# Strassen's seven products for one pair of column chunks of an MLP's down projection

## The chip, the cores and the metric

The kernel runs on one core of a Trainium2 chip. The metric is the device time of one execution in microseconds; of the runs of the kernel before, the median is 2009.23 us (three runs, 2008.05 to 2010.5).

## The reference

A trunk of two layers on 256 tokens of width 2048, in float32. Layer 0 mixes tokens with a gated MLP, layer 1 with sliding-window attention. Each is followed by the MLP that this change touches:

```
def sq_relu_mlp(x, w_up, w_down):        # w_up [2048, 8192], w_down [8192, 2048]
    return jnp.square(jax.nn.relu(x @ w_up)) @ w_down
...
        x = layer_norm(DEEPNORM_ALPHA * x + mix, ln_g[layer, 0], ln_b[layer, 0])
        x = layer_norm(DEEPNORM_ALPHA * x + sq_relu_mlp(x, mlp_w_up[layer], mlp_w_down[layer]),
                       ln_g[layer, 1], ln_b[layer, 1])
```

## The kernel before

**Weights.** All weights come as tiles [128, 1024] of 512 KB in the order of their use, loaded over SP's queue (L119). Each tile is split ahead of its products into two float32r parts: ScalarE rounds it to `w_hi` (L95), VectorE subtracts to get `w_lo` (L97). A product is then three passes on TensorE: high by high, high by low, low by high. There are 4 places for raw tiles (`RAW`) and, in the MLPs, 10 for split ones (`SLOTS` 5 and `EXTRA_SLOTS` 5); near a layer norm four more are borrowed. `get()` takes the next tile, splits as many tiles ahead as have a place and loads the ones after them; `release()` gives a place back when a tile's products are issued. So a split waits for the products that used its place before, and a load for the split that used its raw place.

**One MLP.** The hidden width 8192 is done in four chunks of 2048. For each chunk, the up products come first: 8 blocks of 256 features (`cols_product`, 4 tiles each, weights stationary, 512 and 256 columns moving; L246, L251). Behind each block `act` adds the two column halves (ScalarE L294, VectorE L300), makes the squared ReLU in one VectorE operation (L381) and splits the result into `hT` (ScalarE L185, VectorE L186). Then the down products: for each of four column chunks of 512 (n = 0 to 3) `rows_product` takes 8 tiles, with `hT` stationary and 512 weight columns moving: 12 matmuls a tile, two K tiles by two token tiles by three passes (L205 to L207). Behind it `residual` adds the two PSUM banks to x (VectorE L353). The last column chunk of the last chunk (`last_rows`) runs token tile 0 ahead of tile 1, so that the layer norm overlaps, and the transposes of the norm run into the next stage's first products (`skewed`).

**PSUM.** The eight banks are two tags of two buffers of two banks: `mm` for products, `aux` for transposes and attention.

**Order.** The framework that builds the program puts the instructions of each engine into a fixed order ahead of time, by what it expects to be ready, and the one that the program names first when several are; each engine then works through its list in order. `keep_in_program_order` pins loads, and the splits around the layer norms, to the program's order.

**Wide buffers.** Two buffers [128, 2048] (tag `wide`) hold the vectors of a layer norm; attention uses them too.

The functions that the change touches:

Of the kernel before, what the change touches and what calls it, by code (L numbers as in the profile page):

```python
# [17 lines left out]
P = 128  # L18
# [5 lines left out]
NFC = DFF // D  # L24
# [11 lines left out]
EXTRA_SLOTS = 5  # L36
# [11 lines left out]
class Weights:  # L48
    """The weights in the order of their use: each tile [128, 1024] is loaded and split
    into two float32r parts (high + low = the float32 value) ahead of its products."""  # L50

    def __init__(self, tc, pool, tiles):
        self.tc, self.nc, self.pool, self.tiles = tc, tc.nc, pool, tiles
# [63 lines left out]
    def dma(self, out, in_):  # L117
        """Loads keep the order of the program: what is used first is loaded first."""
        self.tc.keep_in_program_order(self.nc.sync.dma_start(out=out, in_=in_))  # L119

    def get(self, ahead=None):
# [3 lines left out]
        self.load(self.n_split + RAW)  # L125
# [4 lines left out]
    def release(self):  # L130
        """The oldest tile in use has been used."""
# [6 lines left out]
def trunk(ctx: ExitStack, tc: tile.TileContext, t, out):  # L138
# [8 lines left out]

    def tiles_of(name):
# [3 lines left out]
    order = []  # L152
    ends = {}
    for name in ("win_v", "win_u", "wout", "mlp0", "kv", "wq", "wo", "mlp1"):
        tiles = (mlp_order(tiles_of("up" + name[3:]), tiles_of("down" + name[3:]))
                 if name.startswith("mlp") else tiles_of(name))
        if name == "wo":
            # the last heads' rows of the first two chunks come after the other rows of both
            tiles = tiles[0:6] + tiles[8:14] + tiles[6:8] + tiles[14:]
        order += tiles  # L160
        ends[name] = len(order)
    weights = Weights(tc, wpool, order)
    weights.by_pool = range(ends["kv"] + 4, ends["wq"], POOL_EVERY)
# [25 lines left out]
    def row_steps(stat, apart=False):  # L189
        """[tokens, 512] of both token tiles: activations stationary, weights moving.  # L190
        One step for each weight tile and token tile."""
# [6 lines left out]
        def step(i, tok, hi, lo):  # L198
            for j in range(2):
                k = 2 * i + j  # L200
                wh, wl = hi[:, j * 512:(j + 1) * 512], lo[:, j * 512:(j + 1) * 512]
                xh = stat[:, k, tok * P:(tok + 1) * P]
                xl = stat[:, k, S + tok * P:S + (tok + 1) * P]
                first, last = k == 0, k == NK - 1
# [3 lines left out]
        return ps, [partial(step, i) for i in range(NK // 2)]  # L208

    def rows_product(stat):  # L210
        ps, steps = row_steps(stat)
# [78 lines left out]
    def gather_halves(ps, bias=None):  # L290
        """The sum of the two column halves of cols_product (with a bias per feature)."""
# [7 lines left out]
        full = work.tile([P, 2, S], F32, tag="full", name="full")  # L299
# [16 lines left out]
    def norm_rows(acc, stats, g, b, tok, done):  # L316
        """acc = the layer norm of acc, by column chunks; done(chunk) follows each."""
# [19 lines left out]
    def norm_transposed(acc, stats, g, b, xT, tok):  # L337
        """acc = the layer norm of acc, and its transpose goes to xT in parts."""
# [10 lines left out]
    def residual(acc, ps, n, stats, scale, toks=range(NT)):  # L349
        """acc = scale * acc + ps on column chunk n."""  # L350
# [7 lines left out]
    def last_rows(x, stat, stats, scale, norm, norm_turns=True):  # L358
        """The last column chunk before a layer norm: the norm of token tile 0 runs while
        the products of tile 1 do."""  # L360
        ps, steps = row_steps(stat, apart=True)
# [8 lines left out]
    def borrow(tag, first):  # L370
        if first < len(order):
            weights.borrow(big.tile([P, 4, 2, TILE], F32R, tag=tag, name="lent"), first)

    def mlp(x, xT, norm, loads, tags, end):
        """norm(stats, hT, tok) follows the products of a token tile."""
        stats = stats_tile()
        x_tag, h_tag = tags
        for fc in range(NFC):
            def act(c, ps):
                full = gather_halves(ps)  # L380
                nc.vector.scalar_tensor_tensor(out=full, in0=full, scalar=0.0, in1=full,  # L381
                                               op0=ALU.max, op1=ALU.mult)
                split(hT[:, 2 * c:2 * c + 2, 0:S], hT[:, 2 * c:2 * c + 2, S:], full)

            c0 = 0
            if fc == 1:
                loads()
# [4 lines left out]
            hT = big.tile([P, NK, 2 * S], F32R, tag=h_tag, name="hT")  # L392
# [3 lines left out]
            for c in range(c0, NK // 2):  # L396
# [20 lines left out]
    # 0 where key j of the band [previous block | own block] is seen by query i, else NEG  # L417
# [8 lines left out]
    x = big.tile([P, NT, D], F32, tag="xa", name="x")  # L426
    xT = big.tile([P, NK, 2 * S], F32R, tag="A", name="xT")
    with tc.tile_pool(name="gating", bufs=1) as gp:
# [33 lines left out]
        for n in range(4):  # L462
            ps = rows_product(xT)
# [55 lines left out]
    with tc.tile_pool(name="extra0", bufs=1) as extra:  # L519
        weights.lend(extra, ends["mlp0"])  # L520
        borrow("A", ends["wout"])
        for n in range(3):
            residual(x, rows_product(yT), n, stats, ALPHA)
# [282 lines left out]
```

## Time and profile before

| | |
|---|---|
| median of the runs | 2009.23 us |
| the profiled execution's span, first to last instruction | 2008.3 us |
| TensorE busy (matmul) | 1963.9 us, 98%, 10388 matmuls |
| TensorE busy (weight loads) | 1685.8 us, 84% |
| VectorE busy | 1252.5 us, 62% |
| ScalarE busy | 915.5 us, 46% |
| GpSimd busy | 103.1 us, 5% |
| read from HBM | 373.72 MB, mean 187 GB/s |

The profiled execution is one run with the hardware's recorder on. Its span is the time that rows add up to; the median of the timed runs lies 0.9 us above it. PE is TensorE's matmul side and PEld its weight loads, DVE is VectorE, ACT ScalarE, POOL GpSimd, SP the engine that issues the loads. L205 is line 205 of the kernel. A matmul's duration in the rows overlaps its neighbours', so the distance between starts is what one costs.

### The profile page before, as it was taken

To read this page: it belongs to the slowest core of one execution; us is meant where nothing else is said; L and a number is where in the kernel's file an instruction comes from. 1 tells how busy PE (TensorE), PEld (TensorE's weight loads), DVE (VectorE), ACT (ScalarE), POOL (GpSimd) and SP (SyncE) were. 2 spreads that over 40 slices of the span, in tenths; PEclk is the share of its full clock that TensorE was granted. 3 is DMA by queue.
4 is the path that set the end of the run, shared out by engine and by line. 5 is a ranking of instruction groups with operands and counts; after the bars stand their busy time and mean duration, and the time that the engine had idled before them with its cause. 6 is when DMAs were issued, how large, how long until landed. Compare 5 with 4: busy or idle time off the path is not lost.

```text
span 2008.3 us, 26243 instructions
## 1 busy us (share of the span) xinstructions
PE 1963.9 (98%) x10388; PEld 1685.8 (84%) x10388; DVE 1252.5 (62%) x1345; ACT 915.5 (46%) x1138; POOL 103.1 (5%) x63
## 2 busy tenths in 40 slices
PE   9999999999999999999998889999999999999997
PEld 7888888888888888888898878888888888888886
DVE  5676686555554655564778997965555555555555
ACT  5445445434443443443456675444344344434432
POOL 0000010000000000000133310100000000000001
PEclk9999999999999999999998899999999999999999
DMA  9754846666666666655543336566676666665653
GB/s 339 259 186 151 301 143 214 189 197 224 192 192 191 187 189 194 190 184 166 179 137 107 104 106 227 175 208 190 197 228 187 194 189 189 189 194 185 189 157 104
DMA packets 105963, 377.54 MB, mean 188 GB/s; under 512 B 12272, under 2 KB 12912, under 8 KB 105840
## 3 DMA queue, kind: packets, MB, share of 16 engines
q1 hardware_dynamic: 105840, 375.86, 59.4%
q8 instruction: 81, 1.33, 0.3%
q14 instruction: 42, 0.34, 0.0%
HBM read 373.72 MB, written 2.10 MB: 187 GB/s over the span
## 4 chain that ended last, share of the span: by engine, by line
issue 82%; PE 8%; DVE 6%; ACT 2%; POOL 2%; DMA 0%; SPq 0%; POOLq 0%; ACTq 0%; DVEq 0%
PE ps_r L205 2%; PE ps_r L206 2%; PE ps_r L207 2%; DVE w_lo L97 1%; ACT p L623 1%; PE ps_c L242 1%; PE ps_c L251 1%; DVE x L332 0%; DVE swap L544 0%; POOL rstd L313 0%; DVE pT L186 0%; POOL x L328 0%; POOL x L327 0%; DVE qT L697 0%; DVE x L330 0%
## 5 line engine op out<-in xcount | busy, mean ns | idle before, releaser
L97 DVE TENSOR_TENSOR w_lo<-w_raw,w_hi 128x1024 fp32r<-128x1024 f32 (+1 forms) x655 | 803.9, 1231 | 569.7 <-ACT w_hi L95 567.7
L95 ACT CAST w_hi<-w_raw 128x1024 fp32r<-128x1024 f32 (+1 forms) x669 | 701.3, 1051 | 760.3 <-PE ps_r L207 413.4
L205 PE MATMUL ps_r<-w_hi,hT 128*128 128x512 f32 x1024 | 398.5, 389 | 0.0
L207 PE MATMUL ps_r<-w_hi,hT 128*128 128x512 f32 x1024 | 398.5, 389 | 0.0
L206 PE MATMUL ps_r<-w_lo,hT 128*128 128x512 f32 x1024 | 398.4, 389 | 0.0
L246 PE MATMUL ps_c<-yT,w_hi 128*128 128x512 f32 x960 | 337.1, 398 | 0.0
L246 PE MATMUL ps_c<-oT,w_hi 128*128 128x512 f32 x960 | 337.1, 398 | 0.0
L251 PE MATMUL ps_c<-yT,w_lo 128*128 128x256 f32 x992 | 272.5, 281 | 0.0
L251 PE MATMUL ps_c<-oT,w_lo 128*128 128x256 f32 x992 | 272.5, 281 | 0.0
L207 PEld LDWEIGHTS ps_r<-w_hi,hT 128*128 128x128 f32 x1024 | 192.2, 188 | 40.0
L206 PEld LDWEIGHTS ps_r<-w_lo,hT 128*128 128x128 f32 x1024 | 192.2, 188 | 40.0
L205 PEld LDWEIGHTS ps_r<-w_hi,hT 128*128 128x128 f32 x1024 | 192.2, 188 | 39.5
L246 PEld LDWEIGHTS ps_c<-oT,w_hi 128*128 128x128 f32 x960 | 178.7, 188 | 41.8
L246 PEld LDWEIGHTS ps_c<-yT,w_hi 128*128 128x128 f32 x960 | 178.7, 188 | 41.8
L251 PEld LDWEIGHTS ps_c<-yT,w_lo 128*128 128x128 f32 x992 | 187.4, 189 | 2.7
L251 PEld LDWEIGHTS ps_c<-oT,w_lo 128*128 128x128 f32 x992 | 187.4, 189 | 2.7
L300 DVE TENSOR_TENSOR full<-ps_c,part 128x512 f32<-128x512 f32 x73 | 50.5, 691 | 91.5 <-ACT part L294 83.7
L294 ACT COPY part<-ps_c 128x512 f32<-128x512 f32 x72 | 42.2, 587 | 131.2 <-PE ps_c L246 128.5
L242 PE MATMUL ps_c<-hT,w_hi 128*128 128x256 f32 x512 | 97.8, 294 | 0.0
L313 POOL TENSOR_TENSOR rstd<-ve,half 128x1 f32<-128x1 f32 x10 | 9.9, 987 | 1709.1 <-DVE ve L311 1709.1
L246 PE MATMUL ps_c<-xT,w_hi 128*128 128x512 f32 x256 | 90.2, 396 | 0.0
L242 PEld LDWEIGHTS ps_c<-hT,w_hi 128*128 128x128 f32 x512 | 84.4, 203 | 0.4
(141 smaller groups left out, 2026.4 us busy)
## 6 DMA issues: line engine op xcount, KB each, us to landing
w_raw<-in_up SPq DMA_DIRECT2D x256, 512.0 KB, 4.2
w_raw<-in_down SPq DMA_DIRECT2D x256, 512.0 KB, 4.1
w_raw<-in_win_u SPq DMA_DIRECT2D x32, 512.0 KB, 4.0
w_raw<-in_wout SPq DMA_DIRECT2D x32, 512.0 KB, 4.4
w_raw<-in_wq SPq DMA_DIRECT2D x32, 512.0 KB, 3.6
w_raw<-in_wo SPq DMA_DIRECT2D x32, 512.0 KB, 4.0
w_raw<-in_win_v SPq DMA_DIRECT2D x31, 512.0 KB, 6.2
b_ln_g<-in_ln_g SPq DMA_DIRECT2D x8, 512.0 KB, 5.6
```

The costliest lines, as they stand in the source:

```text
L95: nc.scalar.copy(out=hi[:, s], in_=raw[:, s])
L97: sub = engine.tensor_tensor(out=lo[:, s], in0=raw[:, s], in1=hi[:, s].bitcast(F32), op=ALU.subtract)
L205: nc.tensor.matmul(out=ps[tok], lhsT=xh, rhs=wh, start=first, stop=False)
L206: nc.tensor.matmul(out=ps[tok], lhsT=xh, rhs=wl, start=False, stop=False)
L207: nc.tensor.matmul(out=ps[tok], lhsT=xl, rhs=wh, start=False, stop=last)
L242: nc.tensor.matmul(out=ps[:, b, 0:S], lhsT=hi[:, w], rhs=stat[:, k, h * S:(h + 1) * S], start=first and h == 0, stop=last and h == 1)
L246: nc.tensor.matmul(out=ps[:, b, :], lhsT=hi[:, w], rhs=stat[:, k, :], start=first, stop=last)
L251: nc.tensor.matmul(out=ps[:, b, 0:S], lhsT=lo[:, w], rhs=stat[:, k, 0:S], start=False, stop=False)
L294: nc.scalar.copy(out=part, in_=ps[:, :, S:])
L300: nc.vector.tensor_tensor(out=full, in0=ps[:, :, 0:S], in1=part, op=ALU.add)
L313: nc.gpsimd.tensor_tensor(out=rstd, in0=ve, in1=half, op=ALU.pow)
L623: nc.scalar.activation(out=p[:, i, :], in_=p[:, i, :], func=AF.Exp, bias=top[:, i:i + 1], accum_out=den[:, i:i + 1])
```

## The change

Each MLP is now done in seven chunks of the hidden width: six of 1024 and one of 2048. In each of the six, column chunks 0 and 1 of the down projection are made together, by Strassen's method, in one *round*; column chunks 2 and 3 are made by `rows_product` as before, over 8 K tiles in place of 16 (4 weight tiles each). The chunk of 2048 is done as before.

A round multiplies token tiles (2) x K by K x column chunks (2). K is taken in *groups* of 512 rows, two blocks of 256, so a group is a 2 x 2 by 2 x 2 block product: 4 weight tiles. Strassen needs 7 products in place of 8, each of a sum of activation blocks by a sum of weight blocks. The round has two groups and accumulates each of the 7 products over them in a PSUM bank of its own; it takes all buffers of `mm` and `aux`.

- Weights: of the 7 operands of a group, 4 are sums that VectorE makes in place in the raw tiles before the split (Winograd's form: each sum uses the one before). A raw tile stays until its last use. The first group's raw tiles are in the 4 raw places, the second group's in the wide buffers.
- Activations: `act` uses ScalarE's Relu and Square in place of the VectorE operation, then splits the four blocks, makes four sums in three VectorE operations and splits these.
- After a round: banks 3, 5 and 6 are added into x on VectorE; banks 0, 1, 2 and 4 are kept in `held` tiles [128, 4, 512], copied by ScalarE in the MLP's first round and added by VectorE in the later ones. After the sixth chunk's round `strassen_end` adds the held parts into x in 8 operations.
- `EXTRA_SLOTS` goes from 5 to 4, to make room for `held`. The layer norm's vectors are loaded at the start of the last chunk, not of the second.

```diff
-NFC = DFF // D
+CHUNKS = ((1024, 1),) * 6 + ((2048, 0),)
...
-EXTRA_SLOTS = 5
+EXTRA_SLOTS = 4
+STATIONARY = (0, 5, 4, 7, 6, 2, 3)
+HELD = (0, 1, 2, 4)
...
+        self.free_raw = {"w": RAW, "wide": 4}
+        self.pair = None
...
-        n_split = len(self.tiles) if n_split is None else n_split
-        while self.n_split < min(n_split, len(self.tiles)):
+        n_split = len(self.operands) if n_split is None else n_split
+        while self.n_split < min(n_split, len(self.operands)):
             place = self._place(self.n_split)
             if place is None:
                 break
             kind, hi, lo = place
-            self.load(self.n_split + 1)
-            raw = self.raw.pop(self.n_split)
+            at, plus, ended = self.operands[self.n_split]
+            self.load(max(at, plus or 0) + 1)
+            raw = self.raw[at]
+            if plus is not None:
+                nc.vector.tensor_tensor(out=raw, in0=raw, in1=self.raw[plus], op=ALU.add)
             for s in self.pieces(self.n_split):
                 nc.scalar.copy(out=hi[:, s], in_=raw[:, s])
                 engine = nc.gpsimd if self.n_split in self.by_pool else nc.vector
@@ -98,15 +112,32 @@
                                            op=ALU.subtract)
                 if self.in_order:
                     self.tc.keep_in_program_order(sub)
+            for n in ended:
+                self.raw.pop(n)
+                self.free_raw[self.homes[n]] += 1
...
-            raw = self.pool.tile([P, TILE], F32, tag="w_raw", bufs=RAW, name="w_raw")
+            home = self.homes[self.n_raw]
+            if not self.free_raw[home]:
+                break
+            if home == "wide" and self.pair is None and self.free_raw[home] < 2:
+                break
+            self.free_raw[home] -= 1
+            if home == "w":
+                raw = self.pool.tile([P, TILE], F32, tag="w_raw", bufs=RAW, name="w_raw")
+            elif self.pair is None:
+                self.pair = self.wide.tile([P, 2, TILE], F32, tag="wide", name="w_wide")
+                raw = self.pair[:, 0]
+            else:
+                raw, self.pair = self.pair[:, 1], None
...
-        self.load(self.n_split + RAW)
+        self.load(len(self.tiles))
...
+    def add_strassen(new, home):
+        r = len(tiles)
+        tiles.extend(new)
+        homes.extend([home] * 4)
+        operands.extend([(r, None, ()), (r, r + 1, ()), (r + 1, r + 2, (r + 1,)), (r + 2, None, ()),
+                         (r, r + 2, (r + 2,)), (r + 3, None, ()), (r, r + 3, (r, r + 3))])
...
+            for width, rounds in CHUNKS:
+                n_up, n_down = width * D // (P * TILE), width // 256
+                add_tiles(up[:n_up])
+                del up[:n_up]
+                for n in range(rounds):
+                    for g in range(width // 512):
+                        add_strassen(down[:4], ("w", "wide")[g % 2])
+                        del down[:4]
+                for n in range(2 * rounds, 4):
+                    add_tiles(down[:n_down])
+                    del down[:n_down]
...
+    def strassen_round(hT, groups, n, held, first, scale):
+        tiles = [psum.tile([P, 2, 512], F32, tag=tag, name="ps_s")
+                 for tag in ("mm", "aux", "aux", "mm")]
+        banks = [tiles[o // 2][:, o % 2, :] for o in range(7)]
+        for g in range(groups):
+            for o, a in enumerate(STATIONARY):
+                hi, lo = weights.get()
+                for j in range(2):
+                    k = 2 * g + j
+                    wh, wl = hi[:, j * 512:(j + 1) * 512], lo[:, j * 512:(j + 1) * 512]
+                    xh, xl = hT[:, k, 0, a, :], hT[:, k, 1, a, :]
+                    start, stop = k == 0, k == 2 * groups - 1
+                    nc.tensor.matmul(out=banks[o], lhsT=xh, rhs=wh, start=start, stop=False)
+                    nc.tensor.matmul(out=banks[o], lhsT=xh, rhs=wl, start=False, stop=False)
+                    nc.tensor.matmul(out=banks[o], lhsT=xl, rhs=wh, start=False, stop=stop)
+                weights.release()
+        own = {3: (0, 1, ALU.subtract), 5: (0, 0, ALU.add), 6: (1, 0, ALU.add)}
+        for o, bank in enumerate(banks):
+            if o in own:
+                tok, c, op = own[o]
+                a = x[:, tok, (n + c) * 512:(n + c + 1) * 512]
+                nc.vector.scalar_tensor_tensor(out=a, in0=a, scalar=scale, in1=bank,
+                                               op0=ALU.mult, op1=op)
+            elif first:
+                nc.scalar.copy(out=held[:, HELD.index(o), :], in_=bank)
+            else:
+                a = held[:, HELD.index(o), :]
+                nc.vector.tensor_tensor(out=a, in0=bank, in1=a, op=ALU.add)
+        if scale != 1.0:
+            a = x[:, 1, (n + 1) * 512:(n + 2) * 512]
+            nc.scalar.mul(out=a, in_=a, mul=scale)
+    def strassen_end(n, held):
+        m1, m5, m7, m6 = (held[:, i, :] for i in range(4))
+        (x11, x12), (x21, x22) = ([x[:, tok, (n + c) * 512:(n + c + 1) * 512] for c in range(2)]
+                                  for tok in range(NT))
+        for out, a, b, op in ((m6, m6, m1, ALU.subtract), (x11, x11, m1, ALU.add),
+                              (x21, x21, m6, ALU.subtract), (x21, x21, m7, ALU.add),
+                              (m5, m6, m5, ALU.subtract), (x12, x12, m5, ALU.add),
+                              (x22, x22, m5, ALU.add), (x22, x22, m7, ALU.subtract)):
+            nc.vector.tensor_tensor(out=out, in0=a, in1=b, op=op)
...
+    def mlp(x, xT, extra, norm, loads, tags, end):
         stats = stats_tile()
         x_tag, h_tag = tags
-        for fc in range(NFC):
+        helds = {}
+        for fc, (width, rounds) in enumerate(CHUNKS):
+            last = fc == len(CHUNKS) - 1
             def act(c, ps):
+                if not rounds:
+                    full = gather_halves(ps)
+                    nc.vector.scalar_tensor_tensor(out=full, in0=full, scalar=0.0, in1=full,
+                                                   op0=ALU.max, op1=ALU.mult)
+                    split(hT[:, 2 * c:2 * c + 2, 0:S], hT[:, 2 * c:2 * c + 2, S:], full)
+                    return
                 full = gather_halves(ps)
-                nc.vector.scalar_tensor_tensor(out=full, in0=full, scalar=0.0, in1=full,
-                                               op0=ALU.max, op1=ALU.mult)
-                split(hT[:, 2 * c:2 * c + 2, 0:S], hT[:, 2 * c:2 * c + 2, S:], full)
+                nc.scalar.activation(out=full, in_=full, func=AF.Relu)
+                nc.scalar.activation(out=full, in_=full, func=AF.Square)
+                a = full.rearrange("p b (t q) -> p (b t) q", t=NT)
+                split(hT[:, c, 0, 0:4], hT[:, c, 1, 0:4], a)
+                b = work.tile([P, 4, P], F32, tag="part", name="sums")
+                nc.vector.tensor_tensor(out=b[:, 0:2], in0=a[:, 0:4:3],
+                                        in1=a[:, 1:2].to_broadcast([P, 2, P]), op=ALU.subtract)
+                nc.vector.tensor_tensor(out=b[:, 2], in0=a[:, 0], in1=b[:, 1], op=ALU.add)
+                nc.vector.tensor_tensor(out=b[:, 3], in0=b[:, 2], in1=a[:, 2], op=ALU.subtract)
+                split(hT[:, c, 0, 4:8], hT[:, c, 1, 4:8], b)
             c0 = 0
-            if fc == 1:
+            if last:
                 loads()
             if fc == 0:
                 c0 = HEAD_LEAD // 4
                 heads = [col_steps(xT) for _ in range(c0)]
                 skewed([f for _, steps in heads for f in steps], HEAD_LEAD, turn_at=HEAD_TURNS)
-            hT = big.tile([P, NK, 2 * S], F32R, tag=h_tag, name="hT")
+            shape = [P, width // 256, 2, 8, P] if rounds else [P, NK, 2 * S]
+            hT = big.tile(shape, F32R, tag=h_tag, name="hT")
+            stat = by_pairs(hT) if rounds else by_halves(hT)
             if fc == 0:
                 for c in range(c0):
                     act(c, heads[c][0])
-            for c in range(c0, NK // 2):
+            for c in range(c0, width // 256):
                 act(c, cols_product(xT))
                 if c == 2:
                     weights.in_order = False
-            if fc == NFC - 1:
+            if last:
                 borrow(x_tag, end)
-            for n in range(4):
-                st = stats if fc == NFC - 1 else None
-                scale = ALPHA if fc == 0 else 1.0
-                if n == 3 and fc == NFC - 1:
-                    last_rows(x, hT, st, scale, partial(norm, stats, hT), end < len(order))
+            scale = ALPHA if fc == 0 else 1.0
+            for n in range(0, 2 * rounds, 2):
+                first = n not in helds
+                if first:
+                    helds[n] = extra.tile([P, 4, 512], F32, tag=f"held{n}", name="held")
+                strassen_round(hT, width // 512, n, helds[n], first, scale)
+            for n in [n for n in helds if not any(n < 2 * r for _, r in CHUNKS[fc + 1:])]:
+                strassen_end(n, helds.pop(n))
+            for n in range(2 * rounds, 4):
+                st = stats if last else None
+                if n == 3 and last:
+                    last_rows(x, hT, st, scale, partial(norm, stats, hT), end < len(operands))
                 else:
-                    residual(x, rows_product(hT), n, st, scale)
+                    residual(x, rows_product(stat, width // P), n, st, scale)
...
+def strassen_tiles(w):
+    b = w.reshape(-1, 2, 2, P, 2, 512).transpose(0, 2, 4, 3, 1, 5).reshape(-1, 4, P, TILE)
+    return b[:, [0, 1, 3, 2]].reshape(-1, P, TILE)
```

`by_pairs` and `by_halves` only name the place of a K tile in the activations' layout. `own` and `held` follow the list of banks in the order of their products.

## Rows read from the trace of the kernel before

**Rows 1.** The page, part 1: the span; busy time, share, instructions by engine.
```profile
span 2008.3 us, 26243 instructions
PE 1963.9 (98%) x10388; PEld 1685.8 (84%) x10388; DVE 1252.5 (62%) x1345; ACT 915.5 (46%) x1138; POOL 103.1 (5%) x63
```
**Rows 2.** Busy us by stretch: length, each engine with its instructions, clock, DMA share, GB/s.
```profile
340.00:1000.00 660.00, 658.61 (x3301) 557.28 (x3300) 372.03 (x371) 281.39 (x298) 4.27 (x3) 1.00 0.63 191
...
1320.00:1960.00 640.00, 640.00 (x3237) 543.24 (x3236) 353.67 (x351) 272.11 (x288) 0.00 (x0) 1.00 0.62 191
```
**Rows 3.** Waits: engine and line, whom it waited for, us in total, times, longest.
```profile
DVE w_lo L97 <- ACT w_hi L95: 567.7, 398, 5.1
ACT w_hi L95 <- PE ps_r L207: 413.4, 237, 15.3
ACT w_hi L95 <- PE ps_c L246: 241.9, 139, 1.8
...
PE ps_p L639 <- POOL p L629: 7.7, 4, 3.1
```
**Rows 4.** Timeline, TensorE, down products of MLP 0: start us, duration us, instruction.
```profile
759.76 0.39 PE L205 MATMUL ps_r<-w_hi,hT 128*128 128x512 f32 x1
...
767.92 0.39 PE L205 MATMUL ps_r<-w_hi,hT 128*128 128x512 f32 x1
```
**Rows 5.** Timeline, VectorE, the residuals behind three down products.
```profile
752.48 1.28 DVE L353 SCALAR_TENSOR_TENSOR x<-x,ps_r 128x512 f32<-128x512 f32 x2 [0.37 <-PE ps_r L207]
774.24 1.29 DVE L353 SCALAR_TENSOR_TENSOR x<-x,ps_r 128x512 f32<-128x512 f32 x2 [0.41 <-PE ps_r L207]
796.00 1.29 DVE L353 SCALAR_TENSOR_TENSOR x<-x,ps_r 128x512 f32<-128x512 f32 x2 [0.41 <-PE ps_r L207]
```
**Rows 6.** Timeline, VectorE, between two blocks of up products.
```profile
829.68 0.69 DVE L300 TENSOR_TENSOR full<-ps_c,part 128x512 f32<-128x512 f32 x1 [1.26 <-ACT part L294]
...
838.54 1.23 DVE L97 TENSOR_TENSOR w_lo<-w_raw,w_hi 128x1024 fp32r<-128x1024 f32 x1 [1.59 <-ACT w_hi L95]
840.98 0.69 DVE L300 TENSOR_TENSOR full<-ps_c,part 128x512 f32<-128x512 f32 x1 [1.21 <-ACT part L294]
```
**Rows 7.** Groups of instructions by shape, VectorE: busy us, mean ns, idle before.
```profile
L186 DVE TENSOR_TENSOR oT<-o,oT 128x256 fp32r<-128x256 f32 x8 | 3.4, 420 | 2.0 <-ACT oT L185 2.0
```
**Rows 8.** Groups of instructions by shape, ScalarE.
```profile
L95 ACT CAST w_hi<-w_raw 128x1024 fp32r<-128x1024 f32 x667 | 700.1, 1052 | 758.3 <-PE ps_r L207 413.4 <-PE ps_c L246 241.9 <-DMA w_raw<-in_win_v 25.6
L294 ACT COPY part<-ps_c 128x512 f32<-128x512 f32 x72 | 42.2, 587 | 131.2 <-PE ps_c L246 128.5 <-PE ps_c L238 2.6
L185 ACT CAST hT<-full 128x512 fp32r<-128x512 f32 x64 | 39.8, 622 | 32.2 <-DVE full L381 32.2
...
L170 ACT ACT_TABLE_LOAD x1 | 1.3, 1283 | 0.8 <-PEq L798 0.8
L623 ACT ACT_TABLE_LOAD x1 | 1.3, 1283 | 0.0
```
**Rows 9.** Timeline, VectorE, after the layer norm at the start of MLP 0.
```profile
295.96 4.62 DVE L97 TENSOR_TENSOR w_lo<-w_raw,w_hi 128x1024 fp32r<-128x1024 f32 x4
...
317.66 1.23 DVE L97 TENSOR_TENSOR w_lo<-w_raw,w_hi 128x1024 fp32r<-128x1024 f32 x1 [1.61 <-ACT w_hi L95]
```
**Rows 10.** The page, part 6: DMA issues, count, KB each, us to landing.
```profile
w_raw<-in_down SPq DMA_DIRECT2D x256, 512.0 KB, 4.1
```
**Rows 11.** The page, part 5: weight loads of the down products.
```profile
L206 PEld LDWEIGHTS ps_r<-w_lo,hT 128*128 128x128 f32 x1024 | 192.2, 188 | 40.0
```

More of the change, by code (lines that the diff above doesn't have):

```diff
@@ L48, with __init__ @@
 class Weights:
-    def __init__(self, tc, pool, tiles):
-        self.tc, self.nc, self.pool, self.tiles = tc, tc.nc, pool, tiles
+    def __init__(self, tc, pool, wide, tiles, homes, operands):
+        self.tc, self.nc, self.pool, self.wide = tc, tc.nc, pool, wide
+        self.tiles, self.homes, self.operands = tiles, homes, operands
         self.others, self.by_pool = [], ()
@@ L146, in trunk, with add_tiles @@
     psum = ctx.enter_context(tc.tile_pool(name="psum", bufs=2, space=bass.MemoryType.PSUM))
+    tiles, homes, operands = [], [], []
+    ends = {}
+    def add_tiles(new):
+        for w in new:
+            tiles.append(w)
+            homes.append("w")
+            operands.append((len(tiles) - 1, None, (len(tiles) - 1,)))
+    def add_strassen(new, home):
[4 more added lines that the diff above has]
+                         (r, r + 2, (r + 2,)), (r + 3, None, ()), (r, r + 3, (r, r + 3))])
     def tiles_of(name):
@@ L150, in tiles_of @@
         return [w[i] for i in range(w.shape[0])]
-    order = []
-    ends = {}
     for name in ("win_v", "win_u", "wout", "mlp0", "kv", "wq", "wo", "mlp1"):
[L155 to L162, printed above, removed]
+        if name.startswith("mlp"):
+            up, down = tiles_of("up" + name[3:]), tiles_of("down" + name[3:])
+            for width, rounds in CHUNKS:
[10 more added lines that the diff above has]
+        else:
+            some = tiles_of(name)
+            if name == "wo":
+                some = some[0:6] + some[8:14] + some[6:8] + some[14:]
+            add_tiles(some)
+        ends[name] = len(operands)
+    weights = Weights(tc, wpool, bc, tiles, homes, operands)
     weights.by_pool = range(ends["kv"] + 4, ends["wq"], POOL_EVERY)
@@ L186, in split, with by_halves, by_pairs, row_steps @@
         nc.vector.tensor_tensor(out=dst_lo, in0=src, in1=dst_hi.bitcast(F32), op=ALU.subtract)
-    def row_steps(stat, apart=False):
+    def by_halves(x):
+        return lambda k, part, tok: x[:, k, part * S + tok * P:part * S + (tok + 1) * P]
+    def by_pairs(x):
+        return lambda k, part, tok: x[:, k // 2, part, k % 2 * NT + tok, :]
+    def row_steps(stat, apart=False, nk=NK):
         if apart:
@@ L201, in step @@
                 wh, wl = hi[:, j * 512:(j + 1) * 512], lo[:, j * 512:(j + 1) * 512]
-                xh = stat[:, k, tok * P:(tok + 1) * P]
-                xl = stat[:, k, S + tok * P:S + (tok + 1) * P]
-                first, last = k == 0, k == NK - 1
+                xh, xl = (stat(k, part, tok) for part in range(2))
+                first, last = k == 0, k == nk - 1
                 nc.tensor.matmul(out=ps[tok], lhsT=xh, rhs=wh, start=first, stop=False)
@@ L298, in gather_halves @@
                                      bias=bias[:, b:b + 1])
-        full = work.tile([P, 2, S], F32, tag="full", name="full")
+        if full is None:
+            full = work.tile([P, 2, S], F32, tag="full", name="full")
         nc.vector.tensor_tensor(out=full, in0=ps[:, :, 0:S], in1=part, op=ALU.add)
@@ L370, in borrow @@
     def borrow(tag, first):
-        if first < len(order):
+        if first < len(operands):
             weights.borrow(big.tile([P, 4, 2, TILE], F32R, tag=tag, name="lent"), first)
-    def mlp(x, xT, norm, loads, tags, end):
+    def strassen_round(hT, groups, n, held, first, scale):
[23 more added lines that the diff above has]
+                nc.scalar.copy(out=held[:, HELD.index(o), :], in_=bank)
+            else:
+                a = held[:, HELD.index(o), :]
[3 more added lines that the diff above has]
+            nc.scalar.mul(out=a, in_=a, mul=scale)
@@ L529, in norm @@
             norm_transposed(x, stats, *kept, tok)
-        mlp(x, yT, norm, lambda: kept.extend((load_wide("ln_g01"), load_wide("ln_b01"))),
+        mlp(x, yT, extra, norm, lambda: kept.extend((load_wide("ln_g01"), load_wide("ln_b01"))),
             ("B", "A"), ends["mlp0"])
@@ L702, in trunk @@
         stats = stats_tile()
-        both = [row_steps(oT) for _ in range(2)]
+        both = [row_steps(by_halves(oT)) for _ in range(2)]
         for n, tiles in ((0, range(6)), (1, range(6)), (0, range(6, 8)), (1, range(6, 8))):
@@ L727, in norm_out @@
         norm_rows(x, stats, *wide, tok, store)
-    mlp(x, oT, norm_out, lambda: wide.extend((load_wide("ln_g11"), load_wide("ln_b11"))),
+    mlp(x, oT, extra, norm_out, lambda: wide.extend((load_wide("ln_g11"), load_wide("ln_b11"))),
         ("B", "A"), ends["mlp1"])
-def mlp_order(up, down):
-    n_up, n_down = len(up) // NFC, len(down) // NFC
-    order = []
-    for fc in range(NFC):
-        order += up[fc * n_up:(fc + 1) * n_up] + down[fc * n_down:(fc + 1) * n_down]
-    return order
 def row_tiles(w):
@@ L750, in col_tiles, with down_tiles @@
     return w.reshape(k // 512, 4, P, n // 256, 256).transpose(3, 0, 2, 1, 4).reshape(-1, P, TILE)
+def strassen_tiles(w):
+    b = w.reshape(-1, 2, 2, P, 2, 512).transpose(0, 2, 4, 3, 1, 5).reshape(-1, 4, P, TILE)
+    return b[:, [0, 1, 3, 2]].reshape(-1, P, TILE)
+def down_tiles(w):
+    parts, at = [], 0
+    for width, rounds in CHUNKS:
+        rows = w[at:at + width]
+        at += width
+        parts += [strassen_tiles(rows[:, n * 1024:(n + 1) * 1024]) for n in range(rounds)]
+        if rounds < 2:
+            parts.append(row_tiles(rows[:, rounds * 1024:]))
+    return np.concatenate(parts)
 def by_partition(v):
@@ L775, in layout @@
         d[f"up{l}"] = col_tiles(a["mlp_w_up"][l])
-        d[f"down{l}"] = np.concatenate(
-            [row_tiles(a["mlp_w_down"][l][fc * D:(fc + 1) * D]) for fc in range(NFC)])
+        d[f"down{l}"] = down_tiles(a["mlp_w_down"][l])
     d["b_in_v"], d["b_in_u"] = a["a_b_in"][:, D:], by_partition(a["a_b_in"][0, :D])
```

16 lines of the change are left out of this document (8 added, 8 removed).

## The prediction, made before the changed kernel was run

> **What bounds the kernel now.** I read the page first, then busy time by stretches, then the table of waits, then TensorE's and VectorE's rows in order of time inside one MLP. The page shows TensorE busy for 98% of the span and VectorE for 62% [rows 1]. The stretches show that this is no average over unlike stages where the change is made: within the first MLP TensorE is busy 658.6 of 660 us, within the second 640.0 of 640, at full granted clock, while VectorE has 56% and ScalarE 43% [rows 2]. The waits say the same from the other side: ScalarE waits 413 and 242 us for TensorE to give back a weight place, VectorE 568 us for ScalarE, and the longest entry in which TensorE's matmuls wait is 7.7 us, in the attention [rows 3]. In time order the row products run as an even comb: the 36 matmuls from 759.76 to 767.92 us start (767.92 - 759.76)/36 = 0.2267 us apart [rows 4]; the residuals behind them come 21.76 us apart, a product of 8 weight tiles, so 2.72 us a tile [rows 5]. The up products come 11.30 us apart for 4 tiles, 2.825 us a tile [rows 6]. So both MLPs are TensorE-bound, and every matmul taken out there is worth 0.2267 us, provided that nothing else becomes late.
>
> [...]
>
> **What the change removes.** A round takes the place of one pair of column chunks over 1024 rows: 8 tiles of 12 matmuls, 96. Its two groups issue 7 products x 2 K tiles x 3 passes each, 84 in all. The saving is 12 matmuls, 12 x 0.2267 = 2.72 us a round; 84 x 0.2267 = 19.04 us is left. Twelve rounds (six chunks, two MLPs) save 144 matmuls, 32.6 us. Forms, moving width and one weight load per matmul are those of the comb, so I keep its spacing.
>
> **What it adds.** VectorE's cadence is 4.62/4 = 1.15 us for a 1024-column operation with two SBUF inputs [rows 9] and 0.64 us for one of 512 (two in 1.28 [rows 5]). A weight sum is of the first kind: 1.15 us. Per chunk of 1024 rows:
> - 38 operands are split instead of 32 tiles (16 up, 14 Strassen, 8 rows): 43.7 us of VectorE. The 8 weight sums are 9.2.
> - Each of the 4 activation blocks has a gather and two splits (3 x 0.64) and three sums of 256, 128 and 128 columns. A 256-column operation took 0.42 [rows 7], so the sums cost between nothing and 1.26; I take 0.9, near the top because all three are short. That is 2.8 a block, 11.2 in all.
> - Four residuals (2.6) and seven bank evictions (4.5).
>
> The sum is 71.2 us of VectorE against 16 x 2.825 + 8 x 2.72 + 19.04 = 86.0 us of TensorE: 83%. ScalarE has 38 x 1.05 + 4 x (0.59 + 4 x 0.62) = 52.2 us, 61%, pricing Relu and Square as the 512-column cast [rows 8]. No engine but TensorE fills the chunk on average. The loads stay the same bytes (the sums are made on chip), so DMA, which lands a tile in 4.1 us [rows 10], has no more to carry.
>
> **Where it bites: the end of a round.** A product needs its operand every 6 x 0.2267 = 1.36 us, half of a tile's 2.72, and its preparation costs VectorE 1.15 + 4/7 x 1.15 = 1.81 us. Nine places (ten before) carry it over. Count from the round's start, with the lookahead full. VectorE still has operands 9 to 14 to make (6 splits, 4 sums, 11.5 us) and the last activation block (2.8): 14.3 us. Operand 14 is wanted at 13 x 1.36 = 17.7, so TensorE does not starve. But all eight PSUM banks are Strassen's. The rows product that follows needs the pair of banks 0 and 1 back, and each is evicted by VectorE, 2 x 0.64 = 1.28 us, queued behind the splits that were asked for earlier. Four raw places allow four of those splits at once (4.6 us); the fifth has to wait for its load, 4.1 us, and leaves a hole for the evictions. 14.3 + 4.6 + 1.28 = 20.2 against 19.04: TensorE would wait 1.2 us. On the other side VectorE has time before the round: the last 8 up tiles are 22.6 us, and in them 8 splits, 4 sums and two blocks are 19.4. If the spare 3.2 us take one sum ahead (a sum needs no place, only its raw tiles), the tally is 19.05 and the wait nothing. I take 0.8 us, nearer to the first, since VectorE also idles 1.2 to 1.6 us at a time waiting for ScalarE's part [rows 6]. In the first round of each MLP ScalarE makes those evictions (2 x 0.59) and has room; but VectorE comes out of the layer norm and only shows idle time again at 317.66 us [rows 9], about 8 us before where such a round would start, and the extra sums and blocks (4 to 5 us) eat that. I take 1 us each. Loss: 10 x 0.8 + 2 x 1 = 10.0 us.
>
> **What is hidden.** Banks 2 to 6 are not wanted before the next rows product 10.9 us later. The eight operations that put the products together at the end (8 x 0.64 = 5.1 us, once per MLP) and the scaling lie beside the two rows products of that chunk, 43.5/2 = 21.8 us of TensorE with 8 splits (9.2 us) in them. The longer activation (ScalarE 0.59 + 4 x 0.62 + VectorE about 2.8, some 6 us in series) is wanted when group 2 starts, 7 x 1.36 = 9.5 us after the last up product. On SP's queue, the loads behind a raw tile that Strassen holds wait up to seven splits longer; the second group's four tiles go to the wide buffers, so they pass before that, and the next four raw tiles are free before the round begins. If that cover went, it would cost up to one load, 4.1 us a round. The loads of the norm's two vectors move to the last chunk, still some 170 us before use. One place less in the ordinary lookahead (9 for 10) is hidden by the waits of ScalarE for TensorE [rows 3]; beyond it at most a tile, 2.7 us, at each of the three norms.
>
> **The sum.** 2008.3 - 32.6 + 10.0 = 1985.7 us of span. The median run is 0.9 us above the profiled span, so 1986.6.
>
> **Rivals.**
> - *Full cover.* Sums run ahead, evictions find the hole, no waits: 2009.2 - 32.6 = 1976.6. For it: VectorE's 17% left over on average. Against: the demand is bunched in the 19 us of a round.
> - *The evictions queue behind the splits (slower).* If the order fixed for VectorE sets the later rows splits ahead as well, each adds 1.15 us. All eight: 14.3 + 9.2 + 1.28 - 19.04 = 5.7 us in ten rounds, 57 - 32.6 + 2 = +26, 2036. It decides from a wait of 3.06 us a round in ten rounds, that is from two more splits in front (3.5 us, 2014). For it: splits are asked for earlier in the program. Against: the raw tiles for them land late.
> - *The lookahead runs dry.* Each operand that is missing at a round's start costs 1.81 us once the slack of 17.7 - 14.3 = 3.4 (two operands) is gone. Four missing in every round are 3.6 us and push the evictions too: about the whole saving, 2005 to 2020. For it: up tiles with sums leave 3.2 us spare in 22.6. Against: the chunk's 83%.
> - *Table loads.* One load of activation tables took 1.28 us, and Copy, Gelu and Identity shared one [rows 8]. If Relu and Square took a load each, a block would cost ScalarE 2.6 us more, 10.3 a chunk (73%), and the last block would end near 9.5, where group 2 wants it: 1 to 2 us a round, near 2003.
>
> The Trainium skill ("ScalarE: Activation LUTs", Table sets: the hidden batching unit) has relu, copy and identity in every set, which speaks against this rival, and does not list Square there; no row of before shows either function.
>
> **How the numbers follow.** The forecast has a chance of 0.50 with an own range of 1979 to 1994 (waits of 0.2 to 1.4 us), full cover 0.25, evictions behind splits 0.13, a dry lookahead 0.09, table loads 0.03. This kernel's measurement tells apart about 0.2%, 4 us. Faster: forecast, full cover, table loads and a tenth of the rest, 0.80; same 0.06, slower 0.14 from the two queue rivals. The range runs from 1975.5 (full cover, a little less) to 2010, which takes in the milder half of the dry lookahead, leaves the slower cases out and holds a little over 8 in 10.
>
> **What would show it.** Right: 84 matmuls 0.227 us apart in a round, no wait inside it, and at its end a wait of the next rows product for an eviction, of about 1 us, ten times; VectorE near 75% in the MLPs, and two table loads in all. Wrong: waits for weight parts inside a round, evictions over 3 us after bank 1 was full, more table loads, or a comb that spreads when VectorE and TensorE are both full.

## The result: 0.8% slower, and the profile after

The changed kernel took 2026.9 us (median of four runs, 2023.3 to 2028.9) where the kernel before took 2009.9 beside it: 1.0079 of the time, 95% interval 1.0064 to 1.0093. 1986.6 was forecast, with a range up to 2010. The profiled execution's span is 2024.7 us, 16.4 above that of before.

First the page of the changed kernel (part 1), against [rows 1].

```profile
span 2024.7 us, 26597 instructions
PE 1949.3 (96%) x10244; PEld 1670.2 (82%) x10244; DVE 1527.6 (75%) x1749; ACT 1069.5 (53%) x1364; POOL 103.1 (5%) x63
```

The 144 matmuls are gone (10388 to 10244), VectorE has gone from 62% to 75%, and TensorE, which was 98% busy, is 96% busy. The stretches in the two MLPs say where, against [rows 2] (same columns):

```profile
340.00:1000.00 660.00, 645.56 (x3213) 545.22 (x3212) 494.96 (x550) 351.07 (x396) 2.47 (x2) 0.99 0.60 193
1320.00:1960.00 640.00, 623.35 (x3143) 527.59 (x3142) 491.29 (x550) 348.51 (x400) 0.00 (x0) 0.99 0.60 191
```

TensorE was idle for 1.4 us in the first of these stretches before and for none in the second; now 14 and 17 us are idle in them, and the granted clock is 0.99 in place of 1.00. The table of waits names what it waits for, an entry that [rows 3] did not have:

```profile
ACT w_hi L109 <- PE ps_r L274: 208.8, 127, 9.8
...
PE ps_r L272 <- DVE held L472: 31.1, 9, 4.9
```

L272 is the first matmul of the rows product that follows a round, and L472 the addition of a bank into its held part. Nine times it waits. One of them in order of time on TensorE (start, duration, instruction, wait):

```profile
705.26 0.39 PE L459 MATMUL ps_s<-w_hi,hT 128*128 128x512 f32 x1
709.38 0.47 PE L272 MATMUL ps_r<-w_hi,hT 128*128 128x512 f32 x1 [3.74 <-DVE held L472]
709.69 0.54 PE L273 MATMUL ps_r<-w_lo,hT 128*128 128x512 f32 x1
710.03 0.63 PE L274 MATMUL ps_r<-w_hi,hT 128*128 128x512 f32 x1
710.46 0.63 PE L272 MATMUL ps_r<-w_hi,hT 128*128 128x512 f32 x1
...
713.33 0.39 PE L273 MATMUL ps_r<-w_lo,hT 128*128 128x512 f32 x1
713.56 0.40 PE L274 MATMUL ps_r<-w_hi,hT 128*128 128x512 f32 x1
```

Two things are to be seen. The rows product starts 4.12 us after the round's last matmul in place of 0.23. And behind the wait the matmuls start 0.43 us apart and not 0.23, for some eight of them. The stretches around it show why (same columns as above; the eighth figure, before the DMA share, is the granted clock):

```profile
700.00:705.20 5.20, 5.20 (x24) 4.30 (x24) 5.20 (x5) 3.41 (x4) 0.00 (x0) 1.00 0.61 193
709.40:713.00 3.60, 3.60 (x9) 2.81 (x10) 3.46 (x4) 2.20 (x3) 0.00 (x0) 0.55 0.85 273
714.00:718.00 4.00, 4.00 (x19) 3.28 (x18) 3.42 (x5) 2.10 (x2) 0.00 (x0) 1.00 0.62 203
```

After a dense round and 4 us without a matmul most of this stretch runs at the clock's lower level (1.2 GHz); behind it the clock is back at 2.4. So such a wait is paid twice. TensorE's rows give the account of all twelve rounds. Without a wait two rounds start 86.02 us apart (332.59 to 418.61). The loss behind a wait is the distance to the next round less 86.02 and less the wait; for the last round of each MLP, that of the widely spaced matmuls:

| round starts at | wait behind it, us | lost behind the wait, us |
|---|---|---|
| 332.59, 600.40, 1340.81 | none | none |
| 418.61 | 2.53 | 1.66 |
| 508.82 | 3.83 | 1.73 |
| 686.42 | 3.89 | 1.73 |
| 778.06 | 4.82 | 1.7 |
| 1426.83 | 2.26 | 0.14 |
| 1515.25 | 3.56 | 1.70 |
| 1606.53 | 4.78 | 2.18 |
| 1699.51 | 1.82 | 0.08 |
| 1787.43 | 5.03 | 2.0 |
| sum | 32.5 | 12.9 |

Behind the waits of 2.26 and 1.82 us no matmul is spaced by 0.43; the 0.1 lost there is the first spacing (0.31 to 0.34). The rest of the column goes to the clock.

The saving of 32.6 us and 16.4 us more were lost, 49.0 in all: 32.5 in waits, 12.9 behind them, and 3.6 outside the rounds' ends. Where these 3.6 us arise is not shown. The transposes of three layer norms span 1.9, 1.2 and 0.9 us more than before; but in the run with nine places alone (the last one below) they span 4.1 us more in all, and that execution is only 0.6 us longer than before.

Why the evictions are late is seen on VectorE, in the round that starts at 778.06 (the last line is ScalarE's):

```profile
792.08 2.35 DVE L111 TENSOR_TENSOR w_lo<-w_raw,w_hi 128x1024 fp32r<-128x1024 f32 x2
794.35 1.22 DVE L111 TENSOR_TENSOR w_lo<-w_wide,w_hi 128x1024 fp32r<-128x1024 f32 x1
795.49 2.35 DVE L111 TENSOR_TENSOR w_lo<-w_raw,w_hi 128x1024 fp32r<-128x1024 f32 x2
798.04 1.23 DVE L111 TENSOR_TENSOR w_lo<-w_raw,w_hi 128x1024 fp32r<-128x1024 f32 x1 [0.20 <-ACT w_hi L109]
799.19 0.68 DVE L472 TENSOR_TENSOR held<-ps_s,held 128x512 f32<-128x512 f32 x1
800.07 1.22 DVE L111 TENSOR_TENSOR w_lo<-w_raw,w_hi 128x1024 fp32r<-128x1024 f32 x1 [0.20 <-ACT w_hi L109]
801.21 0.68 DVE L472 TENSOR_TENSOR held<-ps_s,held 128x512 f32<-128x512 f32 x1
...
796.97 1.05 ACT L109 CAST w_hi<-w_raw 128x1024 fp32r<-128x1024 f32 x1 [2.76 <-DMA w_raw<-in_down]
```

`w_wide` is the round's last operand, `w_raw` are tiles of the rows products. Bank 0 was full 8 products into the round, at about 788.9. Six rows splits (five in these lines, the first at 787.53) stand in front of its eviction and a seventh in front of bank 1's. VectorE even stands still for 0.20 us twice, for a split whose tile has not come (ScalarE waits 2.76 us for the load of the sixth), with a full bank to evict: its order is fixed, and a hole is of no use unless the order expected it there. All nine rounds with a wait have five to seven rows splits in front of bank 1's eviction; in three of them (418.61, 1426.83, 1699.51) bank 0 is evicted early and bank 1 alone is late. In the one later round without a wait, at 600.40, none stands in front of either bank:

```profile
612.44 1.22 DVE L107 TENSOR_TENSOR w_wide<-w_wide 128x1024 f32<-128x1024 f32 x1
613.58 1.28 DVE L472 TENSOR_TENSOR held<-ps_s,held 128x512 f32<-128x512 f32 x2
614.84 1.23 DVE L111 TENSOR_TENSOR w_lo<-w_wide,w_hi 128x1024 fp32r<-128x1024 f32 x1
```

So the theory (A): the evictions stand behind splits in VectorE's order, and TensorE's wait for them lowers its clock on top. Its rivals: (B) VectorE has too much to do in a round for any order; (C) the seven chunks, the smaller lookahead or the loads cost the time.

### The profile page after: what moved, and what is told of

It reads as the page before. It is cut to its first block, busy times and chain, and to the rows that moved or that the text cites. A ratio compares the mean times of both kernels' runs of the same rounds, so it can differ in the third digit from the quotient of the medians.

```text
span 2024.7 us, 26597 instructions
## 1 busy us (share of the span) xinstructions
PE 1949.3 (96%) x10244; PEld 1670.2 (82%) x10244; DVE 1527.6 (75%) x1749; ACT 1069.5 (53%) x1364; POOL 103.1 (5%) x63
## 4 chain that ended last, share of the span: by engine, by line
issue 82%; PE 8%; DVE 5%; ACT 2%; POOL 1%; DMA 0%; SPq 0%; POOLq 0%; ACTq 0%; DVEq 0%
PE ps_r L274 2%; PE ps_r L272 2%; PE ps_r L273 2%; PE ps_c L309 1%; DVE w_lo L111 1%; ACT p L763 1%; PE ps_c L318 1%; DVE x L400 0%; POOL rstd L381 0%; DVE qT L837 0%; DVE top L754 0%; POOL x L396 0%; DVE es L758 0%; POOL x L395 0%; DMA w_raw<-in_win_v 0%
## 5 line engine op out<-in xcount | busy, mean ns | idle before, releaser
L111 DVE TENSOR_TENSOR w_lo<-w_raw,w_hi 128x1024 fp32r<-128x1024 f32 (+1 forms) x643 | 784.7, 1231 | 340.2 <-ACT w_hi L109 337.6
L109 ACT CAST w_hi<-w_raw 128x1024 fp32r<-128x1024 f32 (+1 forms) x657 | 687.2, 1052 | 581.9 <-PE ps_r L274 208.8
L272 PE MATMUL ps_r<-w_hi,hT 128*128 128x512 f32 x640 | 255.4, 399 | 31.1 <-DVE held L472 31.1
L274 PE MATMUL ps_r<-w_hi,hT 128*128 128x512 f32 x640 | 253.5, 396 | 0.0
L273 PE MATMUL ps_r<-w_lo,hT 128*128 128x512 f32 x640 | 253.4, 396 | 0.0
L272 PEld LDWEIGHTS ps_r<-w_hi,hT 128*128 128x128 f32 x640 | 123.1, 192 | 60.2 <-DVE held L472 18.0
L274 PEld LDWEIGHTS ps_r<-w_hi,hT 128*128 128x128 f32 x640 | 122.9, 192 | 26.3
L273 PEld LDWEIGHTS ps_r<-w_lo,hT 128*128 128x128 f32 x640 | 123.3, 193 | 25.7
L459 PE MATMUL ps_s<-w_hi,hT 128*128 128x512 f32 x336 | 130.9, 389 | 0.0
L458 PE MATMUL ps_s<-w_lo,hT 128*128 128x512 f32 x336 | 130.8, 389 | 0.0
L457 PE MATMUL ps_s<-w_hi,hT 128*128 128x512 f32 x336 | 130.7, 389 | 0.0
L111 DVE TENSOR_TENSOR w_lo<-w_wide,w_hi 128x1024 fp32r<-128x1024 f32 x84 | 101.6, 1222 | 18.0 <-ACT w_hi L109 17.8
L109 ACT CAST w_hi<-w_wide 128x1024 fp32r<-128x1024 f32 x84 | 87.3, 1051 | 27.0 <-PE ps_c L313 15.8
```

The source lines that it names most:

```text
L109: nc.scalar.copy(out=hi[:, s], in_=raw[:, s])
L111: sub = engine.tensor_tensor(out=lo[:, s], in0=raw[:, s], in1=hi[:, s].bitcast(F32), op=ALU.subtract)
L272: nc.tensor.matmul(out=ps[tok], lhsT=xh, rhs=wh, start=first, stop=False)
L273: nc.tensor.matmul(out=ps[tok], lhsT=xh, rhs=wl, start=False, stop=False)
L274: nc.tensor.matmul(out=ps[tok], lhsT=xl, rhs=wh, start=False, stop=last)
L457: nc.tensor.matmul(out=banks[o], lhsT=xh, rhs=wh, start=start, stop=False)
```

## The experiments

**Each eviction named behind its own bank's last product.** The order of the program decides between instructions that are ready, so this was meant to put the evictions ahead of the later splits. `evict` holds the body of the old loop.

```diff
                 weights.release()
+                if g == groups - 1:
+                    evict(o, banks[o])
...
-        for o, bank in enumerate(banks):
...
```

> Edit: each of the seven bank evictions of a round is named right behind the last product of its bank instead of all seven behind the round, so that it stands ahead of the splits asked for later. No operation is added or removed. Theory A (the evictions stand behind four to six rows splits in VectorE's fixed order, and the wait also lowers TensorE's clock): the nine waits of 2.05 to 5.26 us behind the rounds (32.5 us) and the matmuls at 0.43 us spacing behind seven of them (about 1.7 us each, 12 us) go: 2026.9 - 44.5 = about 1982 us. Rival B (VectorE has too much to do in a round, whatever the order): the wait only moves, to weight parts inside the round or the rows product, and the time stays above 2015. Rival C (chunking and the smaller lookahead cost the time): unchanged within 5 us of 2027.

2009.2 us, 0.9991 of before (0.9982 to 1.0000): 18 us better than the change, and not the 45 that theory A gave. It was a miss, and taken alone it spoke for B. TensorE's rows near the end of the round that starts at 777.52 say what happened:

```profile
790.91 0.39 PE L473 MATMUL ps_s<-w_hi,hT 128*128 128x512 f32 x1
792.75 0.51 PE L471 MATMUL ps_s<-w_hi,hT 128*128 128x512 f32 x1 [1.45 <-ACT w_hi L109]
793.41 0.50 PE L471 MATMUL ps_s<-w_hi,hT 128*128 128x512 f32 x1 [0.16 <-DVE held L461]
...
796.28 0.50 PE L272 MATMUL ps_r<-w_hi,hT 128*128 128x512 f32 x1
...
798.24 0.39 PE L471 MATMUL ps_s<-w_hi,hT 128*128 128x512 f32 x1
```

A rows product (L272) starts inside the round and products (L471) follow it: TensorE's own order has changed. A matmul of a product waits for an eviction. These rows suggest that an eviction named between the two products of one PSUM buffer makes the second product wait for it, and that the order then draws other products forward, whose operands are not there yet; the next edit tests it. Over the whole run the rows products still wait 8.5 us for evictions (six times), and the products wait 6.4 us for weight parts and 1.4 for evictions. The edit had changed more than VectorE's order.

**Evictions in pairs**, each pair behind the second product of its buffer; and **banks 0 and 1 alone**, the others behind the round.

```diff
+                if g == groups - 1 and (o % 2 or o == 6):
+                    for b in ((6,) if o == 6 else (o - 1, o)):
+                        evict(b, banks[b])
```
```diff
+                if g == groups - 1 and o == 1:
+                    for b in (0, 1):
+                        evict(b, banks[b])
...
+        for b in range(2, 7):
+            evict(b, banks[b])
```

> Edit: as the early evictions of the run before, but named by the pair of banks that share a buffer, behind the second bank's last product (the single ones made TensorE's own order interleave products, because a bank's eviction stood between the products of its buffer). Theory A (order only: splits in front of the evictions): TensorE's order is that of the change, no wait over 1 us behind a round, no waits inside it: 1980 to 1988 us. Rival B (VectorE is too full in a round for any order): the waits move inside the round, 2005 to 2015 us as with the single evictions.

> Edit: only the evictions of banks 0 and 1, which the next rows product waits for, are named behind their second product; the other five stay behind the round. Theory A: 1978 to 1986 us, as good as or better than all in pairs, since only 1.28 us stands ahead of the last operands. Rival B: 2005 to 2015 us.

1980.8 us, 0.9854 of before (0.9839 to 0.9868), and 1980.6 us, 0.9852 (0.9838 to 0.9867), 46 us better than the change with the same operations on every engine. B is out: the work fits. So is C as the cause of the waits, since both versions keep the seven chunks, the nine places and the loads. In the second one none to three rows splits stand in front of bank 1, where the change had five to seven. VectorE in the last round of the first MLP, with banks 0 and 1 named alone (the round starts at 763.08):

```profile
777.10 2.36 DVE L111 TENSOR_TENSOR w_lo<-w_raw,w_hi 128x1024 fp32r<-128x1024 f32 x2
779.37 1.22 DVE L111 TENSOR_TENSOR w_lo<-w_wide,w_hi 128x1024 fp32r<-128x1024 f32 x1
780.50 1.28 DVE L461 TENSOR_TENSOR held<-ps_s,held 128x512 f32<-128x512 f32 x2
781.70 3.49 DVE L111 TENSOR_TENSOR w_lo<-w_raw,w_hi 128x1024 fp32r<-128x1024 f32 x3
```

Both evictions stand right behind the last operand and end at 781.8, and TensorE goes from the round to the rows product without a wait:

```profile
781.91 0.39 PE L473 MATMUL ps_s<-w_hi,hT 128*128 128x512 f32 x1
782.14 0.39 PE L272 MATMUL ps_r<-w_hi,hT 128*128 128x512 f32 x1
```

The evictions end 0.36 us before that start; in three other rounds of this run the rows product starts 0.06 us late. Over the second MLP its stretch reads:

```profile
1300.00:1940.00 640.00, 640.00 (x3245) 543.21 (x3244) 501.18 (x559) 355.35 (x406) 0.00 (x0) 1.00 0.60 197
```

TensorE has no idle time again, with VectorE at 78%.

**Banks 0 and 1 copied by ScalarE**, added by VectorE later, named behind the round as in the change.

```diff
+        moved = {}
+        if not first:
+            for o, tag in ((0, "part"), (1, "full")):
+                moved[o] = work.tile([P, 512], F32, tag=tag, name="moved")
+                nc.scalar.copy(out=moved[o], in_=banks[o])
...
-                nc.vector.tensor_tensor(out=a, in0=bank, in1=a, op=ALU.add)
+                nc.vector.tensor_tensor(out=a, in0=moved.get(o, bank), in1=a, op=ALU.add)
```

> Edit: behind the ten rounds after an MLP's first, ScalarE copies banks 0 and 1 into work buffers (0.59 us each) and VectorE adds them to the held parts later; named behind the round as in the change. Theory A: VectorE's order no longer matters to the rows product; ScalarE's list has its casts in front instead (1.05 us each, fewer waits): waits of at most 2 us, 1980 to 1995 us. Rival B: as the change without the 1.28 us, 2005 to 2020 us.

1979.9 us, 0.9844 (0.9827 to 0.9860): 0.1 us below what A gave, and no round has a wait behind it. Its second MLP:

```profile
1300.00:1940.00 640.00, 640.00 (x3247) 543.45 (x3246) 500.48 (x560) 360.07 (x416) 0.00 (x0) 1.00 0.60 197
```

It is the same result by another way, since VectorE has as many operations and only the engine that frees the two banks differs. These three versions beat both kernels; their runs can't rank them.

**Without the weight sums.** `nc.vector.tensor_tensor(out=raw, in0=raw, in1=self.raw[plus], ...)` is taken out. The products are then of other weights, and only the time counts.

> Edit: the weight sums are left out (each operand is split from one raw tile as it is, so the products are of other weights); 96 VectorE operations of 1.22 us fewer, evictions named where the change names them. Theory A: in a round 4 sums of the second group go, 4.6 us of VectorE, so the rows splits in front of the evictions are done earlier and the waits of 2 to 5.3 us shrink to 0 to 1 us: about 1985 to 1995 us. Rival B (load): about 1980, with no wait anywhere. Rival C: no change, 2027.

1980.5 us in a single run, at B's figure, with no wait in any round. VectorE, in the round that starts at 762.32:

```profile
773.18 4.63 DVE L109 TENSOR_TENSOR w_lo<-w_raw,w_hi 128x1024 fp32r<-128x1024 f32 x4
777.72 1.28 DVE L470 TENSOR_TENSOR held<-ps_s,held 128x512 f32<-128x512 f32 x2
```

The splits are still in front, but all that stands there is done 2 us before the round ends. So lightening VectorE's list heals it as well as reordering it: the run alone would have led to B, and only the pairs tell that there was room all along.

**Twelve matmuls into the idle bank**, after ten rounds, to keep TensorE at work while it waits.

```diff
+        if not first:
+            for _ in range(12):
+                nc.tensor.matmul(out=tiles[3][:, 1, :], lhsT=hT[:, 0, 0, 0, :],
+                                 rhs=hT[:, 0, 0, 0:4, :].rearrange("p a q -> p (a q)"),
+                                 start=True, stop=True)
```

> Edit: behind each of the ten rounds after an MLP's first, 12 matmuls of 512 columns (2.72 us) into the eighth PSUM bank, which nothing reads; they stand where TensorE waits. Theory A with its second part (a wait that is long enough lowers TensorE's clock, and the next eight matmuls cost 0.43 instead of 0.23 us): no rows product starts at 0.43 us spacing, 12 us come back, the rounds whose wait was shorter than the filler lose 4 us: about 2019 us. If the slow matmuls behind a round come from something else than the idle time (the burst of loads, PSUM evictions beside them): they stay, and the time rises by 4 us to about 2031.

2018.8 us, 1.0043 of before (1.0026 to 1.0059): 8 us better than the change, with added work that nobody uses. TensorE behind the round that starts at 506.21:

```profile
525.27 2.88 PE L463 MATMUL ps_s<-hT 128*128 128x512 f32 x12
529.42 0.47 PE L272 MATMUL ps_r<-w_hi,hT 128*128 128x512 f32 x1 [1.26 <-DVE held L477]
529.73 0.40 PE L273 MATMUL ps_r<-w_lo,hT 128*128 128x512 f32 x1
529.96 0.39 PE L274 MATMUL ps_r<-w_hi,hT 128*128 128x512 f32 x1
```

The rows product starts 0.3 us later in its round than in the change, but at 0.23 us spacing. In two of the ten rounds the spacing of 0.43 stayed, behind idle times of 2.4 and 2.3 us; in a third, 2.3 us idle left the clock as it was. So the clock's part goes with the idle time, not with the loads or the evictions, which are there as before. The size was met partly by luck: at the rounds the clock gives back some 9 us, and filler and waits together take 5 more than the waits did, a gain of 4. The profiled spans differ by 8.7; the other 4.7 lie outside the rounds (1.2 ahead of the first, most of the rest between the two MLPs), and no run shows that the filler made them.

**Seven chunks without a round**, and **nine places in the kernel before**.

```diff
-CHUNKS = ((1024, 1),) * 6 + ((2048, 0),)
+CHUNKS = ((1024, 0),) * 6 + ((2048, 0),)
```
```diff
-EXTRA_SLOTS = 5
+EXTRA_SLOTS = 4
```

> Edit: no Strassen round in any chunk; the seven chunks, 9 places, the new loading and the activation path of a chunk without rounds stay. Theory A: as the kernel before within 5 us (2005 to 2015), since what costs the time is at the rounds. Rival C (chunking, one place fewer, loads): 2020 to 2030, most of the difference to before is here already.

> Edit: the kernel before with 9 places for split weights in the MLPs instead of 10, nothing else. The seven chunks without a round took 1.0013 of the time before. Theory: that small rest is the place that is missing around the layer norms, where ten places are held at once: 1.001 of before here too (about 2 us). Rival: it is the seven chunks: 1.000 here.

2013.1 us, 1.0013 (1.0004 to 1.0023): 2 to 3 us belong to what the change does beside the rounds, and C is out as the cause of the rest. (This run has no loads into the wide buffers; the versions above have them, without waits.) Nine places alone took 2012.6, 1.0008 (0.9999 to 1.0016), which lies between the two answers; whether the 2 to 3 us are the missing place or the chunks stays open.

## Why the prediction was wrong

- **What bounds the kernel and what a matmul is worth: right.** A round's 84 matmuls run from 332.59 to 351.43, 18.84 us for 83 steps, 0.227 each. The fixed versions give back 30 of the 32.6 us.
- **The prices: right.** A weight sum 1.22 us busy (1.15 taken from start to start), the three small sums 0.42 + 0.29 + 0.29 = 1.0 (0.9 taken), Relu and Square 0.63 (0.62), two table loads in all, VectorE 75 and 77% of the two MLP stretches. No round has a wait inside it.
- **The first rounds** cost nothing, for the 1 us each that was taken. [rows 9] was misread there: the trace of before has VectorE idle for 0.79 us ahead of 304.45 already, and the round starts 14.9 us behind the row at 317.66, not 8. The 3.6 us outside the rounds' ends were put at nothing in the sum.
- **The step that failed** is this one: "Four raw places allow four of those splits at once (4.6 us); the fifth has to wait for its load, 4.1 us, and leaves a hole for the evictions." In the round at 778.06 it was the sixth split that waited for its load, 2.76 us on ScalarE, of which 0.20 were left on VectorE, and this hole was not used. The step treated VectorE as if it took whatever was ready, while its list is fixed ahead. Six splits stood in front of bank 0 there and one between the banks; five to seven stood in front of bank 1 in each round with a wait. With six the tally itself holds: 14.3 + 6 x 1.15 = 21.2 us from the round's start to the first eviction, measured 799.19 - 778.06 = 21.1. So 0.8 us a round became 3.25 (32.5/10). The prediction's own sign of being wrong, evictions over 3 us after bank 1 was full, is met: it was full at about 790.3 and evicted from 801.21.
- **A term was missing:** what the clock takes after a wait, most of the 12.9 us. TensorE had no such wait in the MLPs of the kernel before, so its rows there could not show it.
- **The rival that came true** is the one that was given 0.13, the evictions behind the splits. Its mechanism is the one that the runs show. Its size is partly luck: its point of decision, 3.06 us a round, was just passed, and the clock, which it did not have, moved the time from about 2014 to 2026.9, the middle of its 2014 to 2036.

The range ended at 2010, and the place of two operations in VectorE's order decided over 46 us. The tally had put their end at 20.2 or 19.05 against 19.04: the point from which a wait begins, ten times over. That did not allow 0.80 for faster.

## What to carry to other kernels

Where a stage takes all PSUM buffers, name the evictions that the next stage waits for ahead of any preparation for later work, but never between two products that share a buffer. Count a queue by its fixed order, not by what is ready, and read that order in every repetition, because one round in the hoped-for order hides nine late ones. Before judging that an engine is too full, move its instructions: the same work in another order was worth 46 us here, and leaving work out (the weight sums) would, taken alone, have pointed to the wrong cause.

## What the runs showed of the hardware

- A wait of 3.6 to 5.0 us after a dense stretch of matmuls cost 1.7 to 2.2 us more behind it, at the lower level of the clock (0.55 granted in the stretch shown); of the short ones, 2.53 cost 1.66, and 2.26 and 1.82 cost 0.1. The Trainium skill ("TensorE: Matmul & The Clock Gate", HAM oscillation) tells of the same kind of cost for a kernel whose TensorE waits for loads in every K tile and starts the next one at the lower clock. The trace agrees in kind: here the waits are for PSUM evictions, nine in 1300 us of MLPs, and seven of them were followed by matmuls 0.43 us apart.
- Matmuls into a bank that nobody reads, put where TensorE would idle, left the spacing of 0.43 us behind two rounds in place of seven: some 9 us of the clock's part came back, and filler and waits took 5 more. The kernel became 8 us faster, of which the rounds account for 4.
